# Strassen weight sums on VectorE, another order of products and later transposes in a decoder block's feed-forward

## The chip, the cores and the metric

The kernel runs on one core of one Trainium2 chip. The metric is the device time of one execution in microseconds; the time of a kernel is the median of its runs.

## The reference

A decoder block on x of 256 tokens x 2048 channels, all in float32: one input projection, a gated convolution and a gated linear attention, an output projection, a LayerNorm, and then the feed-forward with its own LayerNorm. The change lies in the feed-forward:

```python
x = layer_norm(DN_ALPHA * x + mix, ln1_g[l], ln1_b[l])
ff = jnp.square(jax.nn.relu(x @ w_ff_up[l])) @ w_ff_down[l]
x = layer_norm(DN_ALPHA * x + ff, ln2_g[l], ln2_b[l])
```

w_ff_up is 2048 x 8192, w_ff_down 8192 x 2048.

## The kernel before

**Split products.** Weights come as raw chunks of 512 KB (two blocks of 128 rows by 512 columns; pool rawp, 13 buffers). Each chunk is split into two parts that TensorE multiplies fast: ScalarE casts the high part (L108), VectorE subtracts it from the raw chunk for the low part (L109). The parts lie in one of five split buffers (pool hlp). Every product of two blocks is three matmuls of 512 columns (L153 to L155): high by high, high by low, low by high. Tokens come in two halves t of 128.

**Groups.** The 8192 hidden channels are done in eight groups of 1024. Group 0 is a plain product (`up_first`). Groups 1 to 7 (`up`) are a 2 x 2 Strassen form in Winograd's order: seven products instead of eight, on sums of the tokens' halves (s1, q, s3, s4, made once from x1 while group 0 runs) and sums of the weight quarters r11, r12, r21, r22. Each product has four steps of one weight chunk (28 steps a group, six matmuls a step), and accumulates into one of the PSUM banks a, b, c, d; three of the banks are used by two products, the second adding onto the first.

The list `plan` gives the order: what prepares the weight chunk, the left side, the bank, a DMA that adds to the chunk after its split (`then`), and what follows the last step (`end`). Before, the products come as r11 (bank a), r11+r12 by s1 (c), r21 (a), r11+r12+r22 by q (b), r12+r22 by s3 (d), r22 by s4 (c), r11+r12+r22+r21 (d). Two of the four weight sums are VectorE adds (`first_sum` L719, `third_sum` L724). The other two are made by DMAs from GpSimd's queue that add a weight quarter from HBM onto r11 in SBUF (`plus`, L728, four after the second product, four after the fourth).

**From bank to hidden block.** The `end_` functions combine banks with VectorE into u, v and x (L749, L750, L753, L758, L762), `out` applies relu on ScalarE (L737), `hidden` squares on VectorE (L653), and `put` transposes the block on TensorE (four transposes into a PSUM tile pt, L216) and splits the result into hT for the down product. `lag.soon` holds each such transposition back by a number of steps (two in `up`): `lag.after` is called after each up step and twice in each down chunk, once for each t.

**Down.** Each group's down product is 16 chunks of 12 matmuls; after every fourth chunk VectorE adds the two banks of the pair onto y (L802). Down chunks of the group before run between the up steps. A running count sets how many:

```python
downs, owed = all_downs(), -1.5
for g in range(1, NG):
    hTs.append(t8_pair(f"hT_{g}"))
    for _ in up(g, hTs[g]):
        owed += 4 / 7
        while owed >= 1:
            next(downs)
            owed -= 1
for _ in downs:
    pass
```

So 110 of the 112 down chunks of groups 0 to 6 run between up steps, 2 behind them, and then the last group's 16.

**Order of the work.** The program is traced in the order of the code. A planner with its own estimates of durations then lists each engine's instructions: at each point the earliest traced one that it holds to be ready. On the chip every engine goes through its list in that order. `prepare(s + 1)` stands before the split of step s, so a sum for the next step comes before the low part of this one. Loads all go through SP's queue, each as soon as a raw buffer is free. PSUM has six banks for products and two for transposes; a new tile takes a bank when its readers are done.

Of the kernel before, what the change touches and what calls it, by code (L numbers as in the profile page):

```python
# [12 lines left out]
AF = mybir.ActivationFunctionType  # L13
ALU = mybir.AluOpType
# [9 lines left out]
NB = 512  # L24
# [10 lines left out]
KC = 2  # L35
# [13 lines left out]
FIRST_WAIT = 6  # L49
WAIT_H = 2  # L50
WAIT_C = 8
C_B, C_C, C_U, C_Q, C_K, C_V, C_R, C_Z = 0, 1024, 2048, 3072, 3584, 4096, 5120, 6144

IN_COLS = [(C_Q, NB), (C_K, NB), (C_Z, RANK), (C_V, 2 * NB),
# [5 lines left out]
def hymba_block(ctx, tc, x, x_t, w_in, conv_w, conv_g, w_gate, gate_b, gla_g, w_out,  # L60
                ln1_g, ln1_b, w_up, w_down, ln2_g, ln2_b, out):
    nc = tc.nc
# [54 lines left out]
    def parts_of(raw, ncol, name):  # L117

        pool, tag = homes[0][homes[1] % len(homes[0])]
        homes[1] += 1  # L120
        hl = pool.tile([P, 2, KC, NB], F32R, tag=tag, name=f"hl_{name}")
        split(hl[:, 0, :, :ncol], hl[:, 1, :, :ncol], raw)
        return hl[:, 0], hl[:, 1]

    def piece(w, kt, at, ncol):

        words, n_kt = w
        start = P * (n_kt * at + kt * ncol)
        return words[start:start + P * KC * ncol].rearrange("(p k n) -> p k n", p=P, k=KC)

    def raw_chunk(w, kt, at, ncol, name):
        raw = rawp.tile([P, KC, NB], F32, tag="raw", name=f"raw_{name}")
        load(raw[:, :, :ncol], piece(w, kt, at, ncol))
        return raw[:, :, :ncol]
# [53 lines left out]
    def project(lagged, w, kts, at, ncol, lhs, done, name, ps=None, first=True, last=True,  # L188
                before=None, lags=None):

        ps = {} if ps is None else ps
        n = len(kts) // KC
        for i, chunk in enumerate(weight_chunks(w, kts, at, ncol, name)):
            if before is not None:
                before(i)

            if lags is not None:
                lagged.lag = lags[i]

            def work(t, i=i, chunk=chunk):  # L200
                if t not in ps:
                    ps[t] = acc_tile(f"ps_{name}_{t}")
                mm = products(ps[t], 0, ncol, chunk, lambda kt: lhs(kt, t), first and i == 0, last and i == n - 1)
                if i == n - 1 and last:
                    done(t, ps[t])
                return mm
            lagged.add(work)
        return ps
# [31 lines left out]
    def put(src, pair, j, t, name):  # L240
        transposed(src, pair[0][:, 4 * j:4 * j + 4, t * P:(t + 1) * P],
                   pair[1][:, 4 * j:4 * j + 4, t * P:(t + 1) * P], name)

    def part(pairs, kt, t):
        hi, lo = pairs[kt // 8]
        return hi[:, kt % 8, t * P:(t + 1) * P], lo[:, kt % 8, t * P:(t + 1) * P]
# [4 lines left out]
    with ExitStack() as p1:  # L251
# [97 lines left out]
        first = keep.tile([P, 1], F32, name="first")  # L349
# [127 lines left out]
        def conv_block(j):  # L477
# [26 lines left out]
            def done_b(t, ps):  # L504
# [8 lines left out]
                for g in range(4):  # L513
                    cols = slice(g * P, (g + 1) * P)
                    nc.vector.scalar_tensor_tensor(y[:, cols], y[:, cols], rstd[:, g:g + 1], cg[:, cols],
                                                   op0=ALU.mult, op1=ALU.mult)
                lag0.soon.append([1 + WAIT_C, lambda: put(y, mixT["conv"], j, t, f"c{j}{t}")])

# [29 lines left out]
    with ExitStack() as p2:  # L548
# [99 lines left out]
        def x1lhs(kt, t):  # L648
            return part(x1T, kt, t)

        def hidden(r, hT, i, t, name, wait):

            nc.vector.tensor_mul(r, r, r)  # L653
            lag.soon.append([wait, lambda: put(r, hT, i, t, name)])

        def up_first(hT):

            for i in range(GROUP // NB):
                def done(t, ps, i=i):
                    r = ht.tile([P, NB], F32, tag="relu", name=f"relu_0_{i}_{t}")  # L660
                    nc.scalar.activation(r, ps, AF.Relu)
                    hidden(r, hT, i, t, f"h0_{i}_{t}", 1 + WAIT_H)
                if i == 1:
                    homes[:] = [[(hlp, "hl")], 0]
                    lag.lag = 0
                project(lag, w_up, list(range(KT)), i * NB, NB, x1lhs, done, f"up0_{i}",
                        lags=LAGS if i == 0 else None, before=sums_ahead if i == 1 else None)
# [9 lines left out]
        KH = KT // 2  # L677
# [21 lines left out]
        def of_x1(half, t):  # L699
            return lambda kt: part(x1T, KH * half + kt, t)  # L700

        def of_sum(what):
            return lambda kt: (sums[what][:, 0, kt, :], sums[what][:, 1, kt, :])

        def up(g, hT):

            n1, n2 = g * GROUP, g * GROUP + NB
            r11, r12, r22 = {}, {}, {}

            def raw(at, half, j, name):  # L710
                return raw_chunk(w_up, KH * half + KC * j, at, NB, f"{name}_{g}_{j}")

            def first(j):
                r11[j] = raw(n1, 0, j, "r11")
                return r11[j]

            def first_sum(j):
                r12[j] = raw(n2, 0, j, "r12")
                nc.vector.tensor_add(r11[j], r11[j], r12[j])  # L719
                return r11[j]  # L720

            def third_sum(j):
                r22[j] = raw(n2, 1, j, "r22")
                nc.vector.tensor_add(r12[j], r12[j], r22[j])  # L724
                return r12[j]

            def plus(at):
                return lambda j: nc.gpsimd.dma_start(r11[j], piece(w_up, KH + KC * j, at, NB), accum_op=ALU.add)  # L728

            def tmp(name):  # L730
                return cp.tile([P, NB], F32, tag="c", name=f"{name}_{g}")

            banks, kept = {}, {}

            def out(x, i, t, where=None):
                r = x if where is None else where
                nc.scalar.activation(r, x, AF.Relu)  # L737
                hidden(r, hT, i, t, f"h{g}_{i}_{t}", 2)

            def end_1():  # L740
                kept["p1"] = tmp("p1")
                nc.scalar.copy(kept["p1"], banks["a"])

            def end_2():
                out(banks["a"], 0, 0, ht.tile([P, NB], F32, tag="relu", name=f"relu_{g}"))

            def end_6():
                kept["u"], kept["v"] = tmp("u"), tmp("v")
                nc.vector.tensor_sub(kept["u"], banks["b"], kept["p1"])  # L749
                nc.vector.tensor_sub(kept["v"], banks["c"], kept["u"])  # L750

            def end_7():
                nc.vector.tensor_sub(kept["v"], kept["v"], banks["d"])  # L753
                out(kept["v"], 1, 1)

            def end_3():
                x = tmp("x12")
                nc.vector.tensor_sub(x, kept["u"], banks["c"])  # L758
                out(x, 1, 0)

            def end_4():
                nc.vector.tensor_add(kept["u"], banks["d"], kept["u"])  # L762
                out(kept["u"], 0, 1)

            plan = [(first, of_x1(0, 0), "a", None, end_1),
                    (first_sum, of_sum("s1"), "c", plus(n2), None),
                    (lambda j: raw(n1, 1, j, "r21"), of_x1(1, 0), "a", None, end_2),
                    (lambda j: r11[j], of_sum("q"), "b", plus(n1), end_6),
                    (third_sum, of_sum("s3"), "d", None, end_7),
                    (lambda j: r22[j], of_sum("s4"), "c", None, end_3),  # L770
                    (lambda j: r11[j], of_x1(1, 1), "d", None, end_4)]
            n = KH // KC
            steps = [(p, j) for p in range(len(plan)) for j in range(n)]
            ready = {}

            def prepare(s):
                if s < len(steps):
                    p, j = steps[s]
                    ready[s] = plan[p][0](j)

            prepare(0)
            for s, (p, j) in enumerate(steps):
                _, lhs, bank, then, end = plan[p]
                prepare(s + 1)
                name = f"up{g}_{p}_{j}"
                parts = parts_of(ready.pop(s), NB, name)
                if then is not None:
                    then(j)
                if bank not in banks:
                    banks[bank] = acc_tile(f"ps_up{bank}_{g}")  # L790
                begun = any(q[2] == bank for q in plan[:p])
                mm = products(banks[bank], 0, NB, (list(range(KC * j, KC * j + KC)), *parts), lhs,
                              j == 0 and not begun, j == n - 1, more=begun)
                lag.after(mm)
                if j == n - 1 and end is not None:
                    end()
                yield
# [66 lines left out]
        downs = iter(())  # L864

        def all_downs():
            for g in range(NG - 1):
                yield from down(g, hTs[g])

        downs, owed = all_downs(), -1.5  # L870
        for g in range(1, NG):
            hTs.append(t8_pair(f"hT_{g}"))
            for _ in up(g, hTs[g]):
# [63 lines left out]
```

## Time and profile before

| | us |
|---|---|
| three runs | 1114.16, 1116.71, 1119.34 (median 1116.71) |
| the profiled execution | 1116.4, span 1114.7 |
| VectorE busy | 837.2, 75% of the span |
| ScalarE busy | 598.9, 54% |
| GpSimd busy | 63.9, 6% |
| stretch from the first product of group 1 to the last of group 7 | 440.2 to 1048.1 |

In the rows of the profile, hl_up and hl_dn are split up and down weights, raw_r and raw_dn the raw chunks, ps_upa to ps_upd the up banks, ps_dn the down banks, pt_h the tile of the transposes. PE is TensorE, PEld its weight loads, DVE VectorE, ACT ScalarE, POOL GpSimd, SP the queue of the loads. Rows in order of time have the start and the duration in us, then engine, line and operation; in brackets stands how long the engine sat idle before it and what ended that. Rows of waits have the waiting line, what it waited for, the total in us, the times and the longest. A matmul's duration reaches past the start of the next one, so the distance between starts is what one costs.

### The profile page before, as it was taken

Reading aid. Unit: us, or ns where it says so; the run is one execution under the profiler, and the core shown is the slowest. Engines: PE = TensorE matmul, PEld = TensorE weight load, DVE = VectorE, ACT = ScalarE, POOL = GpSimd, SP = SyncE. Lnnn points to the kernel's source line nnn. Section 1 sums busy time; section 2 is a strip of 40 time slices with the busy share of each in tenths; the row PEclk is TensorE's granted clock in tenths of the full one; section 3 lists DMA queues with packets and bytes.
Section 4 is the critical chain, followed back from the end, with each engine's and each line's share of the span. In section 5 each row is a group of like instructions: output and inputs, shape, how many; then the busy total and the mean of one; then the engine's idle time right before and its main releaser. Section 6 shows DMA issues by size and latency. Waiting matters only on the chain.

```text
span 1114.7 us, 13469 instructions
## 1 busy us (share of the span) xinstructions
PE 1071.6 (96%) x4914; PEld 896.2 (80%) x4914; DVE 837.2 (75%) x958; ACT 598.9 (54%) x695; POOL 63.9 (6%) x74
## 2 busy tenths in 40 slices
PE   9999999999999899999999999999989999989994
PEld 8998888888888778788878877877878877878884
DVE  6555558477655879689789789789879978968867
ACT  6476544436633545556546556556556655645531
POOL 0000000000000110100110110110110110010001
PEclk9999999999999999999999999999999999999998
DMA  9876267676766542997887888788698688688821
GB/s 337 306 254 206 83 209 256 206 225 216 263 225 194 164 159 107 252 258 244 242 228 267 226 228 285 201 239 296 165 252 297 168 251 300 174 232 273 278 63 75
DMA packets 76743, 248.06 MB, mean 223 GB/s; under 512 B 8003, under 2 KB 18259, under 8 KB 76422
## 3 DMA queue, kind: packets, MB, share of 16 engines
q1 hardware_dynamic: 65024, 207.78, 54.7%
q0 software_dynamic: 8064, 29.36, 14.5%
q10 hardware_dynamic: 3590, 10.08, 2.5%
q8 instruction: 38, 0.62, 0.2%
q14 instruction: 27, 0.22, 0.1%
HBM read 244.03 MB, written 3.15 MB: 222 GB/s over the span
## 4 chain that ended last, share of the span: by engine, by line
PE 68%; DVE 14%; DMA 12%; issue 4%; ACT 2%; SPq 0%; DVEq 0%; ACTq 0%
DMA raw_dn<-in_w_ff_down_dram 6%; PE ps_dn L154 6%; PE ps_dn L153 6%; PE ps_dn L155 6%; DMA raw_r<-in_w_ff_up_dram 5%; DVE hl_up L109 5%; DVE hl_dn L109 3%; PE ps_p L155 3%; PE ps_p L153 3%; PE ps_p L154 3%; PE ps_o L155 2%; PE ps_o L154 2%; PE ps_o L153 2%; PE ps_upd L154 2%; PE ps_upd L153 2%
## 5 line engine op out<-in xcount | busy, mean ns | idle before, releaser
L108 ACT CAST hl_up<-raw_r 128x1024 fp32r<-128x1024 f32 x196 | 205.6, 1052 | 107.6 <-PE ps_dn L155 51.5
L109 DVE TENSOR_TENSOR hl_up<-raw_r,hl_up 128x1024 fp32r<-128x1024 f32 x196 | 237.4, 1219 | 30.9 <-ACT hl_up L108 28.4
L108 ACT CAST hl_dn<-raw_dn 128x1024 fp32r<-128x1024 f32 x128 | 134.8, 1053 | 142.8 <-PE ps_dn L155 77.1
L109 DVE TENSOR_TENSOR hl_dn<-raw_dn,hl_dn 128x1024 fp32r<-128x1024 f32 x128 | 156.1, 1220 | 54.4 <-ACT hl_dn L108 53.1
L154 PE MATMUL ps_dn<-hl_dn,hT_hi 128*128 128x512 f32 x496 | 193.5, 390 | 0.5 <-DVE hl_dn L109 0.5
L153 PE MATMUL ps_dn<-hl_dn,hT_hi 128*128 128x512 f32 x496 | 193.3, 390 | 0.0
L155 PE MATMUL ps_dn<-hl_dn,hT_lo 128*128 128x512 f32 x496 | 193.1, 389 | 0.0
L154 PEld LDWEIGHTS ps_dn<-hl_dn,hT_hi 128*128 128x128 f32 x496 | 93.1, 188 | 20.8 <-DVE hl_dn L109 1.3
L153 PEld LDWEIGHTS ps_dn<-hl_dn,hT_hi 128*128 128x128 f32 x496 | 93.1, 188 | 19.8
L155 PEld LDWEIGHTS ps_dn<-hl_dn,hT_lo 128*128 128x128 f32 x496 | 93.1, 188 | 19.4
L728 POOL DMA_DIRECT2D raw_r<-in_w_ff_up_dram x56 | 48.5, 866 | 561.7 <-DVE hl_up L109 530.0
L109 DVE TENSOR_TENSOR hl_p<-raw_p,hl_p 128x824 fp32r<-128x824 f32 (+1 forms) x40 | 40.3, 1016 | 33.4 <-ACT hl_p L108 31.7
L109 DVE TENSOR_TENSOR hl_o<-raw_o,hl_o 128x1024 fp32r<-128x1024 f32 x32 | 38.8, 1222 | 32.9 <-ACT hl_o L108 32.5
L108 ACT CAST hl_o<-raw_o 128x1024 fp32r<-128x1024 f32 x32 | 33.4, 1056 | 45.2 <-PE ps_o L155 31.7
L153 PE MATMUL ps_p<-hl_p,xT_hi 128*128 128x412 f32 (+1 forms) x160 | 56.2, 351 | 0.2 <-ACT xT_hi L108 0.2
L154 PE MATMUL ps_p<-hl_p,xT_hi 128*128 128x412 f32 (+1 forms) x160 | 56.2, 351 | 0.0
L155 PE MATMUL ps_p<-hl_p,xT_lo 128*128 128x412 f32 (+1 forms) x160 | 55.8, 349 | 0.3
L724 DVE TENSOR_TENSOR raw_r<-raw_r,raw_r 128x1024 f32<-128x1024 f32 x28 | 34.2, 1222 | 28.0 <-DMA raw_r<-in_w_ff_up_dram 28.0
L108 ACT CAST hl_p<-raw_p 128x824 fp32r<-128x824 f32 (+1 forms) x40 | 35.1, 885 | 27.1 <-PE ps_p L155 21.4
L154 PE MATMUL ps_upa<-hl_up,x1T_hi 128*128 128x512 f32 x112 | 44.1, 394 | 0.0
L153 PE MATMUL ps_upc<-hl_up,sum_s 128*128 128x512 f32 x112 | 44.1, 394 | 0.0
L153 PE MATMUL ps_upa<-hl_up,x1T_hi 128*128 128x512 f32 x112 | 43.7, 391 | 0.0
(281 smaller groups left out, 2168.2 us busy)
## 6 DMA issues: line engine op xcount, KB each, us to landing
raw_dn<-in_w_ff_down_dram SPq DMA_DIRECT2D x128, 512.0 KB, 5.0
raw_r<-in_w_ff_up_dram SPq DMA_DIRECT2D x112, 512.0 KB, 5.3
raw_r<-in_w_ff_up_dram POOLq DMA_DIRECT2D x56, 512.0 KB, 8.1
raw_o<-in_w_out_dram SPq DMA_DIRECT2D x32, 512.0 KB, 3.5
raw_p<-in_w_in_dram SPq DMA_DIRECT2D x24, 412.0 KB, 5.7
raw_c<-in_w_in_dram SPq DMA_DIRECT2D x16, 512.0 KB, 3.7
raw_u<-in_w_in_dram SPq DMA_DIRECT2D x16, 512.0 KB, 4.3
raw_b<-in_w_in_dram SPq DMA_DIRECT2D x16, 512.0 KB, 4.2
```

The source lines that it names most:

```text
L108: queued("act", lambda: nc.scalar.copy(hi, src))
L109: queued("dve", lambda: nc.vector.tensor_sub(lo, src, hi.bitcast(F32)))
L153: nc.tensor.matmul(ps[:, :ncol], ah, whi[:, j, cols], start=f, stop=False, skip_group_check=more)
L154: nc.tensor.matmul(ps[:, :ncol], ah, wlo[:, j, cols], start=False, stop=False, skip_group_check=more)
L155: nc.tensor.matmul(ps[:, :ncol], al, whi[:, j, cols], start=False, stop=e, skip_group_check=more)
L724: nc.vector.tensor_add(r12[j], r12[j], r22[j])
L728: return lambda j: nc.gpsimd.dma_start(r11[j], piece(w_up, KH + KC * j, at, NB), accum_op=ALU.add)
```

## The change

- The accumulating DMAs (`plus`) are gone. The second and fourth weight sum become VectorE adds: `second_sum` adds r22 onto r11, `fourth_sum` adds r21. VectorE makes 16 adds a group instead of 8.
- The products come in another order: r11 (a), r11+r12 by s1 (c), r12+r22 by s3 (d), r11+r12+r22 by q (b), r22 by s4 (c), r21 (a), r11+r12+r22+r21 (d). `end_7` is merged into `end_6`, which now runs after the fourth product; `end_2` runs after the sixth.
- Where a block lies in SBUF, relu and square are one VectorE instruction (the larger of x and 0, times x) in place of a ScalarE relu and a VectorE multiply. Where it comes straight from a bank (`end_2` and group 0), both are done by ScalarE.
- Transposes in `up` wait six calls instead of two.
- The running count of the down chunks starts at -6 instead of -1.5: 105 chunks run between up steps, 7 behind them. In group 1 the first follows step 13 instead of step 5. In the groups after it down chunks follow steps 1, 2, 4, 6, 8, 9, 11, 13, 15, 16, 18, 20, 22, 23, 25 and 27.

```diff
+WAIT_UP = 6
+BEHIND = 6
...
-        def hidden(r, hT, i, t, name, wait):
-            nc.vector.tensor_mul(r, r, r)
+        def hidden(r, x, hT, i, t, name, wait):
+            if r is x:
+                nc.vector.scalar_tensor_tensor(r, x, 0.0, x, op0=ALU.max, op1=ALU.mult)
+            else:
+                nc.scalar.activation(r, x, AF.Relu)
+                nc.scalar.activation(r, r, AF.Square)
             lag.soon.append([wait, lambda: put(r, hT, i, t, name)])
...
-                    nc.scalar.activation(r, ps, AF.Relu)
-                    hidden(r, hT, i, t, f"h0_{i}_{t}", 1 + WAIT_H)
+                    hidden(r, ps, hT, i, t, f"h0_{i}_{t}", 1 + WAIT_H)
...
-            def plus(at):
-                return lambda j: nc.gpsimd.dma_start(r11[j], piece(w_up, KH + KC * j, at, NB), accum_op=ALU.add)
+            def second_sum(j):
+                nc.vector.tensor_add(r11[j], r11[j], r22[j])
+                return r11[j]
+
+            def last(j):
+                r21[j] = raw(n1, 1, j, "r21")
+                return r21[j]
+
+            def fourth_sum(j):
+                nc.vector.tensor_add(r11[j], r11[j], r21[j])
+                return r11[j]
...
             def out(x, i, t, where=None):
-                r = x if where is None else where
-                nc.scalar.activation(r, x, AF.Relu)
-                hidden(r, hT, i, t, f"h{g}_{i}_{t}", 2)
+                hidden(x if where is None else where, x, hT, i, t, f"h{g}_{i}_{t}", WAIT_UP)
...
                 nc.vector.tensor_sub(kept["u"], banks["b"], kept["p1"])
                 nc.vector.tensor_sub(kept["v"], banks["c"], kept["u"])
-
-            def end_7():
                 nc.vector.tensor_sub(kept["v"], kept["v"], banks["d"])
                 out(kept["v"], 1, 1)
...
-            plan = [(first, of_x1(0, 0), "a", None, end_1),
-                    (first_sum, of_sum("s1"), "c", plus(n2), None),
-                    (lambda j: raw(n1, 1, j, "r21"), of_x1(1, 0), "a", None, end_2),
-                    (lambda j: r11[j], of_sum("q"), "b", plus(n1), end_6),
-                    (third_sum, of_sum("s3"), "d", None, end_7),
-                    (lambda j: r22[j], of_sum("s4"), "c", None, end_3),
-                    (lambda j: r11[j], of_x1(1, 1), "d", None, end_4)]
+            plan = [(first, of_x1(0, 0), "a", end_1),
+                    (first_sum, of_sum("s1"), "c", None),
+                    (third_sum, of_sum("s3"), "d", None),
+                    (second_sum, of_sum("q"), "b", end_6),
+                    (lambda j: r22[j], of_sum("s4"), "c", end_3),
+                    (last, of_x1(1, 0), "a", end_2),
+                    (fourth_sum, of_x1(1, 1), "d", end_4)]
...
-        downs, owed = all_downs(), -1.5
+        downs, owed = all_downs(), -BEHIND
```

More of the change, by code (lines that the diff above doesn't have):

```diff
@@ L707, in up @@
             n1, n2 = g * GROUP, g * GROUP + NB
-            r11, r12, r22 = {}, {}, {}
+            r11, r12, r21, r22 = {}, {}, {}, {}
             def raw(at, half, j, name):
@@ L782, in up @@
             for s, (p, j) in enumerate(steps):
-                _, lhs, bank, then, end = plan[p]
+                _, lhs, bank, end = plan[p]
                 prepare(s + 1)
@@ L786, in up @@
                 parts = parts_of(ready.pop(s), NB, name)
-                if then is not None:
-                    then(j)
                 if bank not in banks:
```

## The prediction

> **What bounds the kernel now.** I read the page's busy shares first, then the waits of TensorE and VectorE in the stretch where up groups 1 to 7 run between the down chunks (440 to 1048 us), then that stretch in one row, then the instructions around one stall in order of time.
>
> ```profile
> PE 1071.6 (96%) x4914; PEld 896.2 (80%) x4914; DVE 837.2 (75%) x958; ACT 598.9 (54%) x695; POOL 63.9 (6%) x74
> L728 POOL DMA_DIRECT2D raw_r<-in_w_ff_up_dram x56 | 48.5, 866 | 561.7 <-DVE hl_up L109 530.0
> q0 software_dynamic: 8064, 29.36, 14.5%
> ...
> PE pt_h L216 <- DVE relu L653: 17.7, 7, 3.8
> PE pt_h L216 <- DVE v L653: 2.3, 4, 0.7
> PE ps_dn L154 <- DVE hl_dn L109: 0.5, 2, 0.3
> ...
> DVE hl_dn L109 <- ACT hl_dn L108: 43.4, 33, 5.3
> DVE raw_r L724 <- DMA raw_r<-in_w_ff_up_dram: 28.0, 17, 3.0
> DVE hl_up L109 <- ACT hl_up L108: 27.8, 26, 2.3
> ...
> ACT hl_dn L108 <- PE ps_dn L155: 57.5, 41, 1.9
> ACT hl_up L108 <- PE ps_dn L155: 51.5, 39, 1.7
> ```
>
> TensorE bounds the stretch, with VectorE some way behind. TensorE is never held by missing weights to speak of (0.5 us); it is held once per group, seven times, by the transposes of the first finished block (end_2's), which wait for VectorE's squaring at L653: 17.7 us in all, the longest 3.8. VectorE's own largest waits are for ScalarE's casts, and these wait for TensorE to free a split buffer: that is back-pressure, not a limit. Only the 28.0 us of L724 are a real lack: r22 has not landed.
>
> The stretch in one row (us, then busy PE, PEld, DVE, ACT, POOL with counts, granted clock, DMA share, GB/s), and TensorE in order of time around one stall, in a dense run, and after a slightly shorter stall:
>
> ```profile
> 440.20:1048.10 607.90, 587.46 (x2603) 481.51 (x2602) 504.40 (x504) 352.37 (x369) 48.49 (x56) 0.99 0.82 240
> ...
> 559.10 0.39 PE L155 MATMUL ps_dn<-hl_dn,hT_lo 128*128 128x512 f32 x1
> 561.95 1.03 PE L216 MATMUL pt_h<-ident,relu 128*128 128x128 f32 x4 [2.46 <-DVE relu L653]
> 562.63 0.78 PE L153 MATMUL ps_upb<-hl_up,sum_q 128*128 128x512 f32 x1
> 565.34 0.44 PE L153 MATMUL ps_upb<-hl_up,sum_q 128*128 128x512 f32 x1
> ...
> 570.88 0.39 PE L153 MATMUL ps_dn<-hl_dn,hT_hi 128*128 128x512 f32 x1
> 589.92 0.39 PE L153 MATMUL ps_upc<-hl_up,sum_s 128*128 128x512 f32 x1
> 590.60 0.63 PE L216 MATMUL pt_h<-ident,v 128*128 128x128 f32 x4
> 591.53 0.39 PE L155 MATMUL ps_upc<-hl_up,sum_s 128*128 128x512 f32 x1
> ...
> 911.40 0.63 PE L216 MATMUL pt_h<-ident,relu 128*128 128x128 f32 x4 [2.33 <-DVE relu L653]
> 911.79 0.48 PE L153 MATMUL ps_upb<-hl_up,sum_q 128*128 128x512 f32 x1
> 913.96 0.39 PE L153 MATMUL ps_upb<-hl_up,sum_q 128*128 128x512 f32 x1
> ```
>
> Between 570.88 and 589.92 lie 84 products (four down chunks of 12, six up chunks of 6): 0.2267 us from start to start. An up chunk is 1.36 us, a down chunk 2.72. Four transposes delay what follows by 0.47 (from 590.60 the third product starts after 0.93 instead of 0.45). So the stretch holds 7 x 28 x 6 + 110 x 12 = 2496 products, 565.8 us, and 28 sets of transposes, 13.2: 579.0 us of work. The rest of its 607.9 is 28.9: 17.7 + 2.3 + 0.5 = 20.5 waited and 8.4 left. Where the 8.4 are is seen after the stall of 2.46: six products from 562.63 to 565.34 took 2.71 us instead of 1.36, half speed. After the stall of 2.33 nine products took 2.17 (0.24 each): full speed. So a stall from about 2.4 us costs some 1.7 us more, one of 2.3 nothing.
>
> The Trainium skill (TensorE: Matmul & The Clock Gate, "HAM oscillation") puts the limit at idle gaps of more than about 3.4 us. The rows differ: 2.46 us was enough. By the page only the 3.8 us stall would be charged and a new stall under 3.4 us would be free: the sum below would lack its 1.7, 1103 instead of 1105.
>
> **The change, part by part.**
>
> *Transposes later, squares elsewhere.* The block that stalls now (end_2) gets relu and square from ScalarE, so VectorE's queue is out of its chain, and all transposes come six products' steps later (some 8 us of TensorE work) instead of two. ScalarE is at 352 of 607.9 us; one square more per group and three relus fewer cost nothing there. In up_first four squares move the same way, beside the products: nothing. The stalls and half-speed windows go: at most 28.9 us.
>
> *56 accumulating DMAs out, 56 adds in.* POOL loses its only work in the stretch. SP issues the same 112 loads: r22 comes two products earlier and r21 three later, past down loads on the same queue. Held raw buffers are 8 to 9 of 13 in products two to four, as they are now. 29.4 MB and q0's 14.5% of the DMA engines go. VectorE is what pays. Its pitch in a dense run:
>
> ```profile
> 612.00 1.22 DVE L719 TENSOR_TENSOR raw_r<-raw_r,raw_r 128x1024 f32<-128x1024 f32 x1
> 613.14 1.22 DVE L109 TENSOR_TENSOR hl_dn<-raw_dn,hl_dn 128x1024 fp32r<-128x1024 f32 x1
> 614.27 0.68 DVE L109 TENSOR_TENSOR hT_lo<-pt_h,hT_hi 128x512 fp32r<-128x512 f32 x1
> 614.87 1.21 DVE L109 TENSOR_TENSOR hl_up<-raw_r,hl_up 128x1024 fp32r<-128x1024 f32 x1
> 616.01 1.22 DVE L719 TENSOR_TENSOR raw_r<-raw_r,raw_r 128x1024 f32<-128x1024 f32 x1
> 617.27 1.23 DVE L109 TENSOR_TENSOR hl_up<-raw_r,hl_up 128x1024 fp32r<-128x1024 f32 x1
> ```
>
> An instruction over 1024 columns takes 1.135 us of the engine (start to start), one over 512 takes 0.60; durations overlap by 0.08. New VectorE work: 504.4 + 56 x 1.135 = 63.6, less 7 multiplies (4.2), and less 5 down chunks that leave the stretch (below; 5.7 + 1.2): 556.9 us. The three fused max-and-multiply per group take the place of three multiplies of the same size: nothing.
>
> *Down chunks later.* The count starts at -6 instead of -1.5, so 105 chunks instead of 110 run inside the stretch and 7 instead of 2 behind it. Total TensorE work is the same; the stretch falls to 579.0 - 5 x 2.72 = 565.4 and 13.6 go behind it, where VectorE needs 1.135 of every 2.72 us. Cost: none by itself. But in group 1 the first down chunk now follows step 13, so products two and three run alone: VectorE needs 2 x 1.135 for each 1.36 of TensorE, 8 x 0.91 = 7.3 us short, against a lead of five split buffers, 6.8. I take 3 us (0.5 if the lead is whole, 7.3 if none).
>
> *The order of products.* This is the part that can bite. Product five (s4) now accumulates into bank c directly behind product four, and end_6 must first read c (v = c - u, after u = b - p1). Today bank c is touched again only eight steps later. Between product four and five stands one down chunk (after step 16). Where u and v stand today, three of the seven groups (last product into b, then u, then v):
>
> ```profile
> 574.73 0.39 PE L155 MATMUL ps_upb<-hl_up,sum_q 128*128 128x512 f32 x1
> 577.27 0.68 DVE L749 TENSOR_TENSOR u<-ps_upb,p 128x512 f32<-128x512 f32 x1
> 579.27 0.68 DVE L750 TENSOR_TENSOR v<-ps_upc,u 128x512 f32<-128x512 f32 x1
> ...
> 746.54 0.39 PE L155 MATMUL ps_upb<-hl_up,sum_q 128*128 128x512 f32 x1
> 750.94 0.68 DVE L749 TENSOR_TENSOR u<-ps_upb,p 128x512 f32<-128x512 f32 x1
> 752.67 0.68 DVE L750 TENSOR_TENSOR v<-ps_upc,u 128x512 f32<-128x512 f32 x1
> ...
> 1014.06 0.39 PE L155 MATMUL ps_upb<-hl_up,sum_q 128*128 128x512 f32 x1
> 1015.40 0.68 DVE L749 TENSOR_TENSOR u<-ps_upb,p 128x512 f32<-128x512 f32 x1
> 1017.37 0.68 DVE L750 TENSOR_TENSOR v<-ps_upc,u 128x512 f32<-128x512 f32 x1
> ```
>
> TensorE would want bank c at 0.23 + 2.72 us after the last row of b; v ends 2.3, 3.9 and 1.05 us after that. If the down chunk covered all, the cost would be 0; as today, 1.05 to 3.9 us per group, with half speed on top from 2.4. I take 1.05: the larger two stand behind L724 adds that waited for DMA, at the very place where the accumulating DMAs ran. 7 x 1.05 = 7.4, and one half-speed window, 1.7. Behind the waiting product five stand all TensorE's later products; VectorE meanwhile refills its lead. Four up banks are now live in product four, so a new pair of down banks (step 13) needs the old pair's adds within 4.1 us; the u row of 746.54 (3.9 + 0.68) says 0 to 0.5 per group. I take 0.
>
> **The sum.** By TensorE: 565.4 + 7.4 + 1.7 + 3 = 577.5. By VectorE: 556.9, plus hand-overs of 0.12 as at 616.01 (1.26 instead of 1.135) on about one in five of 400 long instructions, 10, plus a third of L724's DMA waits, 10, plus waits for b and c, 3: 580. The two stand so close that each pays some of the other's waits; an estimate of 3 more gives 583. With the 13.6 behind the stretch it is 596.6 against 607.9: 11.3 us less. The profiled execution took 1116.4 us (span 1114.7), the median of the runs is 1116.71, so both give **1105 us**.
>
> **Rivals.**
>
> *Nothing takes the stalls' place.* The down chunk covers v and VectorE keeps up: 579.0 in all, 1116.4 - 28.9 = 1087.5, up to 1095 with some of the terms. For it: no accumulating DMAs. Against: VectorE at 556.9 of 565.4, 98%.
>
> *The stall moves from the transposes to bank c.* v late as in the 574.73 and 746.54 rows: 7 x 2.7 = 19, four half-speed windows 7, group 1's 3: 565.4 + 29 + 13.6 = 608, no change, 1111 to 1122. For it: two of three rows. Against: they follow DMA waits.
>
> *VectorE becomes the bound: slower.* It decides from the point where VectorE idles 607.9 - 13.6 - 556.9 = 37 us in the stretch; today it idles 103.5, of which 28.0 for DMA and the rest mostly back-pressure, which goes when its lead is gone. If the DMA waits stay (28) with hand-overs (10) and waits for b (7 x 0.95 as in the 1014.06 rows, 7), it idles 45: 1116.4 + 8 = 1124, and more where loads come later.
>
> The Trainium skill (VectorE: DVE Perf Modes, "The DRAIN you can't avoid") speaks for this one: the next operation would start only when the pipe is empty. By that rule each would cost its whole duration: with 413 long ones (196 + 105 splits, 112 adds) and some 138 short ones, 413 x 1.22 + 138 x 0.68 = 598 us, and with the 13.6 the change would give 1120. The rows above differ: starts lie 1.13 to 1.14 apart under durations of 1.22.
>
> **Chances.** My forecast (1095 to 1111) 0.42; nothing takes the stalls' place 0.16; the stall moves to bank c 0.22; VectorE bounds 0.20. Half a per cent, 5.6 us, is about what a measurement of this kernel can tell from no change. Faster by more: 0.42 + 0.16 = 0.58; within: 0.21; slower: 0.21. Range 1090 to 1122: it cuts a part of the first rival's low end and the slow rival's upper part.
>
> **What would show it.** No POOL DMAs, 56 more long VectorE instructions, DVE near 95% in the stretch; no TensorE wait for relu at the transposes; instead a wait of the first product of ps_upc in product five on v (L750 of today), about 1 us, seven times; DMA share well under 0.82. Wrong would be: that wait over 2.4 us with half-speed products behind it; TensorE waiting for hl_up or hl_dn many times (VectorE bounds); adds waiting for r12 or r22 as long as L724 does now.

## The result and the profile after

| | before | after |
|---|---|---|
| median of 4 runs, us | 1116.68 | 1087.12 (1086.87 to 1087.62) |
| ratio | | 0.9737, 95% interval 0.9719 to 0.9755 |
| profiled execution, us | 1116.4, span 1114.7 | 1086.87, span 1085.1 |
| granted clock, mean | 0.988 | 0.995 |
| stretch of groups 1 to 7, us | 607.9 | 567.4 |

29.6 us less, where 11 were forecast; the time lies below the range. It is near the first rival, "nothing takes the stalls' place" (1087.5).

Of two kernels below ("the same, with later transposes" and "2 long VectorE instructions more a group") the one profiled execution took over 3000 us: the ratios leave it out, and no rows of these two are shown.

From the page after, the busy shares and the one queue of the loads (GpSimd's has no transfers left); from its waits, the longest of TensorE's (it lies in LayerNorm 1, ahead of the stretch) and VectorE's two largest in the stretch; and the stretch in one row (us, busy PE, PEld, DVE, ACT, POOL with counts, clock, DMA share, GB/s). Line numbers are two or more higher than before; L111 is L109 of before.

```profile
PE 1062.4 (98%) x4914; PEld 892.2 (82%) x4914; DVE 888.8 (82%) x1003; ACT 594.0 (55%) x685; POOL 15.4 (1%) x18
q1 hardware_dynamic: 65024, 207.78, 58.2%
...
PE pt_x L218 <- DVE y L595: 2.8, 1, 2.8
...
DVE hl_up L111 <- ACT hl_up L110: 8.9, 7, 1.5
DVE hl_dn L111 <- ACT hl_dn L110: 4.8, 7, 1.2
...
440.13:1007.56 567.43, 567.29 (x2554) 468.38 (x2552) 549.87 (x545) 342.09 (x354) 0.00 (x0) 1.00 0.62 202
```

Not one wait of TensorE is left in the stretch: it is busy 567.29 of 567.43 us at full clock. VectorE does 45 instructions more and is at 97%. No add waits for a DMA. The stretch is 40.5 us shorter, and what follows it is 10.9 longer (77.5 against 66.6). The prediction moved five down chunks behind the stretch, 13.6 us; it was four, because in the trace of before the stretch holds 109 chunks (1308 down products up to the last up product) and not the 110 of the program. The stretch after is 2.0 us longer than the 565.4 of pure work that the prediction counted.

Bank c, the place that the prediction feared, in group 2 of the kernel after (last product into b, the first one behind it, first product of s4; u and v on VectorE):

```profile
552.57 0.39 PE L157 MATMUL ps_upb<-hl_up,sum_q 128*128 128x512 f32 x1
552.80 0.39 PE L155 MATMUL ps_dn<-hl_dn,hT_hi 128*128 128x512 f32 x1
556.20 0.39 PE L155 MATMUL ps_upc<-hl_up,sum_s 128*128 128x512 f32 x1
...
553.42 0.68 DVE L761 TENSOR_TENSOR u<-ps_upb,p 128x512 f32<-128x512 f32 x1
555.15 0.68 DVE L762 TENSOR_TENSOR v<-ps_upc,u 128x512 f32<-128x512 f32 x1
```

v ends at 555.83, 3.03 us after TensorE could have gone on; 15 down products stand between (3.40 us), three more than the one chunk that the program's order puts there: the planner listed some earlier. Over the seven groups v ends 2.6 to 3.1 us after that point, and the products between take 2.9 to 3.4.

### The profile page after: what moved, and what is told of

It is laid out like the page before. It is cut to its first block, busy times and chain, and to the rows that moved or that the text cites. A ratio compares the mean times of both kernels' runs of the same rounds, so it can differ in the third digit from the quotient of the medians.

```text
span 1085.1 us, 13282 instructions
## 1 busy us (share of the span) xinstructions
PE 1062.4 (98%) x4914; PEld 892.2 (82%) x4914; DVE 888.8 (82%) x1003; ACT 594.0 (55%) x685; POOL 15.4 (1%) x18
## 4 chain that ended last, share of the span: by engine, by line
PE 91%; DVE 6%; ACT 1%; DMA 1%; issue 1%; DVEq 0%
PE ps_dn L156 10%; PE ps_dn L157 10%; PE ps_dn L155 10%; PE ps_p L157 3%; PE ps_p L156 3%; PE ps_p L155 3%; PE ps_o L157 2%; PE ps_o L156 2%; PE ps_o L155 2%; PE ps_upa L155 2%; PE ps_upc L155 2%; PE ps_upa L157 2%; PE ps_upa L156 2%; PE ps_upc L156 2%; PE ps_upc L157 2%; PE ps_upd L155 2%
## 5 line engine op out<-in xcount | busy, mean ns | idle before, releaser
L111 DVE TENSOR_TENSOR hl_up<-raw_r,hl_up 128x1024 fp32r<-128x1024 f32 x196 | 236.8, 1218 | 9.8 <-ACT hl_up L110 9.3
L111 DVE TENSOR_TENSOR hl_dn<-raw_dn,hl_dn 128x1024 fp32r<-128x1024 f32 x128 | 156.0, 1219 | 22.5 <-ACT hl_dn L110 21.6
L111 DVE TENSOR_TENSOR hl_p<-raw_p,hl_p 128x824 fp32r<-128x824 f32 (+1 forms) x40 | 40.3, 1017 | 33.1 <-ACT hl_p L110 31.4
L111 DVE TENSOR_TENSOR hl_o<-raw_o,hl_o 128x1024 fp32r<-128x1024 f32 x32 | 38.8, 1223 | 32.8 <-ACT hl_o L110 32.5
L155 PE MATMUL ps_upc<-hl_up,sum_s 128*128 128x512 f32 x112 | 44.3, 396 | 0.0
L157 PE MATMUL ps_upa<-hl_up,x1T_lo 128*128 128x512 f32 x112 | 43.7, 390 | 0.0
L156 PE MATMUL ps_upc<-hl_up,sum_s 128*128 128x512 f32 x112 | 43.7, 390 | 0.0
```

Source lines behind the costliest of these rows:

```text
L111: queued("dve", lambda: nc.vector.tensor_sub(lo, src, hi.bitcast(F32)))
L155: nc.tensor.matmul(ps[:, :ncol], ah, whi[:, j, cols], start=f, stop=False, skip_group_check=more)
L156: nc.tensor.matmul(ps[:, :ncol], ah, wlo[:, j, cols], start=False, stop=False, skip_group_check=more)
L157: nc.tensor.matmul(ps[:, :ncol], al, whi[:, j, cols], start=False, stop=e, skip_group_check=more)
```

## The experiments

All times are medians in us; ratios are to the kernel before on the same chip.

| kernel | us | ratio, 95% interval |
|---|---|---|
| before + spacing alone | 1119.27 | 1.0017 (1.0000 to 1.0034) |
| before + squares alone | 1132.21 | 1.0111 (1.0075 to 1.0146) |
| before + spacing and squares, old order | 1119.46 | 1.0030 (1.0009 to 1.0052) |
| after, sums 2 and 4 by DMA again | 1087.21 | 0.9721 (0.9707 to 0.9736) |
| after, old spacing | 1092.11 | 0.9767 (0.9752 to 0.9781) |
| after, square of end_2 on VectorE | 1089.00 | 0.9747 (0.9733 to 0.9762) |
| after, no down chunk traced between products four and five | 1087.67 | 0.9735 (0.9718 to 0.9752) |
| after, 2 long VectorE instructions more a group | 1089.16 | 0.9745 (0.9728 to 0.9761) |
| after, 6 more a group | 1116.10 | 0.9992 (0.9982 to 1.0003) |
| after, 11 raw buffers | 1091.45 | 0.9767 (0.9743 to 0.9792) |
| before, no accumulating DMAs | 1087.16 | 0.9729 (0.9708 to 0.9751) |
| the same, with later transposes | 1086.85 | 0.9727 (0.9703 to 0.9752) |
| before, only the four behind product two | 1110.39 | 0.9938 (0.9922 to 0.9955) |
| before, only the four behind product four | 1097.85 | 0.9825 (0.9810 to 0.9840) |
| before, the 56 as plain loads | 1088.02 | 0.9737 (0.9723 to 0.9752) |

**Spacing alone.** In the kernel before:

```diff
-                hidden(r, hT, i, t, f"h{g}_{i}_{t}", 2)
+                hidden(r, hT, i, t, f"h{g}_{i}_{t}", 6)
-        downs, owed = all_downs(), -1.5
+        downs, owed = all_downs(), -6
```

> The kernel before with only the spacing changed: transposes six calls later instead of two, down chunks counted from -6 instead of -1.5. Order of products, accumulating DMAs and squares as before. Theory A (the gain is the end of the seven stalls at end_2's transposes, and the spacing alone ends them): TensorE's 20.5 us of waits and 8.4 us of half speed go, 1088 to 1092 us. Theory B (VectorE ran late because of the accumulating DMAs, and only their removal ends the stalls): VectorE's adds at L724 still wait about 28 us for DMAs, and half or more of the stall stays, 1100 to 1112 us.

**Squares alone.** `hidden` and `out` of the change, all else as before.

> The kernel before with only relu and square changed: one VectorE instruction for the blocks in SBUF, ScalarE for both where a block comes from a bank. Spacing two calls, order and DMAs as before. Theory A2 (the stall is VectorE's queue in front of end_2's square; ScalarE's square would end 0.6 us after its relu, which is before TensorE asks for it): the wait of 17.7 us falls below 3 and nearly all half speed goes, 1089 to 1096 us. Theory A (only the spacing ends the stalls): the wait moves to ScalarE and stays above 1 us a group, 1103 to 1115 us.

**Spacing and squares, in the old order** with the accumulating DMAs: the whole change without its order and sums.

> The changed kernel's squares, spacing and down count, but the order of products and the accumulating DMAs of before: all of the change except order and sums. Spacing alone gave 1119 us and squares alone 1132; the new order with the sums left to the DMAs 1087. Theory C (r22 lands late in the old order and TensorE stalls behind VectorE's L724 wherever that shows): 1115 to 1130 us, L724 waiting 30 us or more for DMAs. Theory A, saved (both spacing and squares are needed to end the stall): 1087 to 1095 us.

1119, 1132 and 1119 us: none gains, and in the first two neither theory's time was met. TensorE's and VectorE's waits in the stretch (waiting line, what for, us in total, times, longest), of the three in turn, with ScalarE's wait for down loads in the second:

```profile
PE ps_dn L154 <- DVE hl_dn L109: 21.3, 8, 5.9
DVE raw_r L724 <- DMA raw_r<-in_w_ff_up_dram: 48.9, 20, 8.2
...
PE pt_h L216 <- DVE v L654: 13.2, 7, 2.1
PE ps_upb L154 <- DVE hl_up L109: 11.8, 7, 2.2
DVE raw_r L727 <- DMA raw_r<-in_w_ff_up_dram: 36.4, 21, 3.6
ACT hl_dn L108 <- DMA raw_dn<-in_w_ff_down_dram: 79.5, 17, 8.9
...
PE ps_dn L154 <- DVE hl_dn L109: 20.3, 11, 5.6
DVE raw_r L727 <- DMA raw_r<-in_w_ff_up_dram: 53.5, 25, 7.9
```

The transposes no longer stall (with spacing), and the same 20 us stand elsewhere in the group, where TensorE runs out of split weights. With spacing alone each of the seven long stalls (1.6 to 5.9 us) comes 2.4 us after an L724 add that waited 4.0 to 8.2 us for r22. So the stall at the transposes was only the place where VectorE's lateness showed; what made VectorE late was still there. Theory A fell; the saved form of it, that both edits together are needed, fell with the third run. With the squares alone TensorE stalls at two places a group: 2.4 us after an L727 add (L724 of before) that waited 3.2 to 3.6 us for r22, and, from group 1 to 6, some 12 us after a cast that waited 7.0 to 8.9 us for a down load. ScalarE waits 79.5 us for down loads in that run, 47.3 in the kernel before. Why these loads come so much later there stays open.

**The new order, with the two sums left to the DMAs.** In the kernel after:

```diff
-                    (first_sum, of_sum("s1"), "c", None),
+                    (first_sum, of_sum("s1"), "c", plus(n2), None),
...
-                    (second_sum, of_sum("q"), "b", end_6),
+                    (lambda j: r11[j], of_sum("q"), "b", plus(n1), end_6),
...
-                    (fourth_sum, of_x1(1, 1), "d", end_4)]
+                    (lambda j: r11[j], of_x1(1, 1), "d", None, end_4)]
```

> The changed kernel with the second and fourth weight sum made by accumulating DMAs again, issued behind the splits of products two and four; all else as changed (order of products, spacing, squares). VectorE has 56 long instructions fewer (63.6 us). Theory A (VectorE at 550 of 567 us was no bound, and DMAs were no bound before): 1086 to 1090 us, as the changed kernel. Theory B: the accumulating DMAs bring TensorE stalls back, above 1095 us.

1087.21, as the kernel after. The stretch (row of 440.13 to 1007.56 as above), VectorE's wait for r22 and ScalarE's for down loads in this run:

```profile
440.13:1007.56 567.43, 567.43 (x2555) 468.31 (x2554) 494.20 (x488) 340.60 (x355) 48.53 (x56) 1.00 0.85 254
...
DVE raw_r L729 <- DMA raw_r<-in_w_ff_up_dram: 16.9, 6, 4.2
ACT hl_dn L110 <- DMA raw_dn<-in_w_ff_down_dram: 29.4, 8, 5.9
```

TensorE never waits in the stretch, although VectorE still waits 16.9 us for r22, ScalarE 29.4 for down loads, and the DMA engines are at 0.85. The down loads even take longer to land than in the kernel before (median 6.4 us against 5.1 between 440 and 1010). So in this order late loads cost nothing, and VectorE's adds brought nothing and cost nothing. Why this order bears them is not shown. VectorE has 56 us less to do here than in the kernel after, which leaves it time to catch up, but hardly less than in the kernel before (494.2 against 504.4). The new spacing and squares are in this run too; the new order with accumulating DMAs and without them was not run.

**The accumulating DMAs left out, in the old order.** These kernels leave r22 and r21 out of r11's sums; they show what the DMAs cost. Before, with old spacing and squares, then with later transposes and down chunks counted from -6:

```diff
-                if then is not None:
-                    then(j)
```

> The kernel before with its 56 accumulating DMAs left out, so that r22 and r21 are missing from r11's sums; all else, the old order too, as before. Theory D (the DMA engines are too full where r22 is loaded): L724's waits for DMA fall from 28.0 us to a few, the stalls at end_2's transposes to a third, 1088 to 1098 us. Theory E (r22 is late because of its place in the old order, with 13 raw buffers of which r11, r12 and r21 hold 8 to 10): the waits stay above 15 us, 1105 to 1117 us.

> The same without the accumulating DMAs, with transposes six calls later and down chunks counted from -6. Theory D: no DMA wait and no early transposes are left, 1086 to 1090 us. Theory E: L724's waits stay near the 48.9 us that the later transposes alone showed, 1108 to 1119 us.

1087.16 and 1086.85. With the old order, the old spacing and the old squares, the whole gain is there once these 56 DMAs are gone. The window of before's stretch (440.20 to 1048.10; in this run it also takes in work from behind the stretch, which ends some 30 us earlier) and the waits, of the first of the two:

```profile
440.20:1048.10 607.90, 607.90 (x2737) 501.21 (x2737) 524.84 (x528) 367.28 (x382) 0.00 (x0) 1.00 0.62 200
...
DVE raw_r L724 <- DMA raw_r<-in_w_ff_up_dram: 2.6, 7, 0.6
...
ACT hl_dn L108 <- DMA raw_dn<-in_w_ff_down_dram: 2.2, 4, 0.5
```

The last row is the one that was missed. In the kernel before it reads:

```profile
ACT hl_dn L108 <- DMA raw_dn<-in_w_ff_down_dram: 47.3, 23, 5.5
```

Theory D holds in its main point: without these DMAs the loads are in time and the stalls go. Its other point, that it is the load of r22 which counts, is taken up by the next runs. Theory E falls.

**Which of them, and why.** Only the four behind product two (r21 is missing from r11's sums), only the four behind product four (r22 is missing), and all 56 as plain loads, which overwrite r11:

```diff
 (first_sum, of_sum("s1"), "c", plus(n2), None)     # only these four: plus(n1) -> None
 (lambda j: r11[j], of_sum("q"), "b", plus(n1), end_6)   # only these four: plus(n2) -> None
...
-... piece(w_up, KH + KC * j, at, NB), accum_op=ALU.add)
+... piece(w_up, KH + KC * j, at, NB))
```

> The kernel before with only the first four accumulating DMAs of each group (r22 onto r11 behind product two); the four that add r21 behind product four are left out of the computation. If those behind product four are the ones in the way (they are issued while r22 is loaded for L724): L724's waits fall below 5 us, 1086 to 1090 us. If the first four are: 1105 us or more.

> The kernel before with only the second four (r21 onto r11 behind product four); the four behind product two are left out of the computation. If these are the ones in the way: L724 still waits 15 us or more for DMAs and TensorE stalls at end_2's transposes, 1105 to 1117 us. If it takes both sets: 1087 to 1098 us.

> The kernel before with the 56 DMAs from GpSimd's queue as plain loads into r11 that overwrite it, so r11's sums are not made. If what hurts is the adding (reading and writing SBUF beside the bytes from HBM): they take about half the DMA engines' time, L724's waits fall below 10 us, 1087 to 1095 us. If it is the 29 MB, or GpSimd's queue as such: 1110 to 1118 us.

Waits of TensorE, VectorE and ScalarE with the first four only, then with the second four only:

```profile
PE pt_h L216 <- DVE relu L653: 17.2, 7, 3.4
DVE raw_r L724 <- DMA raw_r<-in_w_ff_up_dram: 10.6, 7, 2.1
ACT hl_dn L108 <- DMA raw_dn<-in_w_ff_down_dram: 29.9, 14, 5.2
...
PE pt_h L216 <- DVE v L653: 5.2, 7, 1.0
DVE raw_r L724 <- DMA raw_r<-in_w_ff_up_dram: 27.9, 20, 3.6
ACT hl_dn L108 <- DMA raw_dn<-in_w_ff_down_dram: 22.0, 12, 3.5
```

My expectation was the wrong way round: L724's 27.9 us of waits come with the second four, where TensorE waits 6.8 us (5.2 at the transposes, 1.6 for hl_dn) and the run is about 10 us longer than with plain loads. The stall at end_2's transposes comes with the first four, with 10.6 us at L724; TensorE waits 17.2 us, and the run is about 22 us longer. They act in another way. In the kernel before, one group (the load's issue on SP's queue, ScalarE's cast of that chunk, VectorE's split of it):

```profile
537.86 0.33 SPq L112 DMA_DIRECT2D raw_dn<-in_w_ff_down_dram  x1
...
546.83 1.05 ACT L108 CAST hl_dn<-raw_dn 128x1024 fp32r<-128x1024 f32 x1 [3.93 <-DMA raw_dn<-in_w_ff_down_dram]
...
547.91 1.22 DVE L109 TENSOR_TENSOR hl_dn<-raw_dn,hl_dn 128x1024 fp32r<-128x1024 f32 x1 [3.76 <-ACT hl_dn L108]
```

A down load issued at 537.86, among four accumulating DMAs (issued from 530.91 to 539.27), takes 8.7 us to land and is used at 546.83; ScalarE stands 3.93 us and behind it VectorE 3.76, and 14 us later the square that end_2's transposes need comes 2.46 us late. It is so in all seven groups: such a wait of ScalarE, 2.1 to 5.5 us, lies some 15 us ahead of the stall, and the longer it is the longer the stall (1.70 us behind the shortest, 3.82 behind the longest). Between the two lies a wait of L724 of 1.2 to 1.9 us; what each contributes was not separated. What slows the load (page of before, then of the run with plain loads: issues on GpSimd's queue with us to landing, and that queue's packets, MB and share of the DMA engines; before's share, 14.5%, stands in the prediction):

```profile
raw_r<-in_w_ff_up_dram POOLq DMA_DIRECT2D x56, 512.0 KB, 8.1
...
raw_r<-in_w_ff_up_dram POOLq DMA_DIRECT2D x56, 512.0 KB, 4.9
q0 software_dynamic: 8064, 29.36, 8.4%
```

The same 29.36 MB from the same queue as plain loads take 8.4% of the engines instead of 14.5% and cost next to nothing (1088.02 against 1087.16 without them). It is the adding, not the bytes or the queue. How the adding delays the other loads inside the DMA engines no run shows. The Trainium skill (DMA: Bandwidth & Descriptors, "SWDGE vs HWDGE vs iDMA") ties accumulating transfers to GpSimd's queue; what they do to plain loads beside them is measured by these runs.

**Was bank c covered by luck?** Down chunks counted from -6.5, so that none is traced between product four and five:

```diff
-BEHIND = 6
+BEHIND = 6.5
```

> The changed kernel with the down chunks counted from -6.5 instead of -6: again 105 inside the stretch, but they follow steps 15 and 17 and not 16, so product five follows product four directly. v was done 3.0 us after the last product into bank b could have been followed. If the down chunk between the two was what covered v: seven stalls of about 3 us and half speed after most of them, 1108 to 1122 us. If the planner puts other products there: 1087 to 1092 us.

1087.67. Last product into b, next product, first one of s4:

```profile
553.55 0.39 PE L157 MATMUL ps_upb<-hl_up,sum_q 128*128 128x512 f32 x1
553.78 0.39 PE L155 MATMUL ps_dn<-hl_dn,hT_hi 128*128 128x512 f32 x1
557.63 0.39 PE L155 MATMUL ps_upc<-hl_up,sum_s 128*128 128x512 f32 x1
```

17 down products stand between, where the program's order has none. The planner fills the gap.

**How much room has VectorE?** The low part subtracted twice at some steps of each group:

```diff
+                if s in (0, 18):    # or (0, 5, 10, 15, 20, 25)
+                    nc.vector.tensor_sub(parts[1], src, parts[0].bitcast(F32))
```

> The changed kernel with the low part of a split subtracted twice in 2 of the 28 steps of each group (steps 0 and 18): 14 long VectorE instructions more, 15.9 us. VectorE then has 549.9 + 15.9 = 565.8 us of work in a stretch of 567.4. If VectorE's limit is its work by the distance between starts (1.135 us each), with nearly no idle: 1087 to 1092 us. If each instruction costs its whole duration, VectorE already was the bound and each one adds 1.22: 1104 us. By the prediction's 23 us of idle that VectorE can't avoid: about 1108 us.

> The same with the low part subtracted twice in 6 of 28 steps (0, 5, 10, 15, 20, 25): 42 long instructions more, 47.7 us, VectorE 597.6 us against TensorE's 567.4. If VectorE bounds from there on: 1087 + 30 = 1117 us, up to 1128 with short TensorE stalls that are charged with half speed. If its lead and the stretches around it take up part: 1105 to 1115 us.

1089.16 and 1116.10: 14 instructions more (15.9 us by 1.135 each) cost about 2, 42 (47.7 us) cost 29. With six more a group VectorE is the bound, busy all the time (TensorE has 579.91 of the same stretch):

```profile
440.10:1035.00 594.90, 579.91 (x2550) 465.14 (x2549) 591.63 (x584) 335.24 (x353) 0.00 (x0) 1.00 0.56 189
```

VectorE idled 17.6 us in the stretch of after (567.43 less 549.87); 47.7 less 17.6 is 30, near the 29 measured. So VectorE's limit is its work at 1.135 us per long instruction, and in this run it was filled to 99% (591.63 of 594.90).

**Spacing, squares and buffers in the new order.**

> The changed kernel with the old spacing: transposes two calls later, down chunks counted from -1.5. By theory A2 end_2 stays without a stall, but v's four VectorE instructions end 6.3 us after product four (they are spread over four splits) and its transposes are asked for after about 2.7 us; and with this count no down chunk stands between product four and five, so bank c is asked for 3.0 us before v has read it. 3.5 to 6 us per group and half speed on top: 1112 to 1135 us. If the planner fills both gaps with down products: 1087 to 1095 us.

> The changed kernel with the square of end_2 (and of group 0) on VectorE again, behind ScalarE's relu; spacing of six calls and all else as changed. Theory A (the spacing ends the stall, whoever squares): 1086 to 1090 us. If it was the square on ScalarE: a wait for VectorE of 1 us or more per group, above 1093 us.

> The changed kernel with 11 raw buffers instead of 13. Theory E (what counts is how many raw buffers are left for loads ahead): with 3 instead of 5 beside the 8 held ones, loads of r12 and r22 come late, VectorE waits for DMAs 20 us or more, 1095 to 1125 us. Theory D (bandwidth, which is at 0.62 here): 1087 to 1091 us.

With the old spacing (`WAIT_UP = 2`, `BEHIND = 1.5`) the new order takes 1092.11 instead of 1087.12: the transposes of u wait six times.

```profile
PE pt_h L218 <- DVE u L656: 4.1, 6, 1.3
```

The stalls expected at v and bank c (25 us or more) are not there; the planner filled them. With the squares of end_2 and of group 0 on VectorE it is 1089.00, with no TensorE wait above 1 us in the stretch. Neither edit is where the gain came from; in the new order the spacing is worth some 5 us. With 11 raw buffers the time is 1091.45: ScalarE waits 41.1 us for down loads (0.6 in the kernel after), but TensorE under 2 us in the stretch. So two buffers less cost about 4 us and not the 8 or more that theory E needs; where the rest of the 4 us goes was not followed.

## Why the prediction was wrong

- **The step of the sum that failed.** The sum went by VectorE: 580 us, and 3 more for mutual waiting, 583 for the stretch. It took 567.4, and TensorE was busy in all but 0.14 of them. VectorE's work was put at 556.9 us; 549.9 was measured, for nearly the same count (546 instructions worked out, 545 in the row). The 23 us of idle time added to it (hand-overs 10, waits for DMA 10, waits for b and c 3) were 17.6, the mutual waiting of 3 was nothing, and none of it held TensorE. TensorE's own line was too high as well, by the 12.1 us put down for bank c and group 1.
- **What bounds the kernel now.** The 28.9 us of waits and half speed were near the 29.6 that went. But I read VectorE's 43.4 us of waits for ScalarE's casts as back-pressure by quoting only ScalarE's waits for TensorE. ScalarE's 47.3 us for down loads stand in the same view and lead to the same stall. "Only the 28.0 us of L724 are a real lack" is the reading that failed, and with it the mechanism: the idle terms and bank c were priced by rows of before, in which late loads held VectorE.
- **Transposes later, squares elsewhere: the stalls go.** They went, by another edit. Spacing and squares gain nothing in the old order. What freed the kernel is either leaving out the accumulating DMAs in the old order (1087.16) or the new order, with new spacing and squares, in spite of them (1087.21).
- **56 DMAs out, 56 adds in.** I kept a third of L724's waits, 10 us, although the DMAs go; no add waits for a DMA in the stretch. That the DMAs themselves cost the old order some 30 us (ratio 0.9729 without them) is nowhere in the sum.
- **The order of products.** 7 x 1.05 and 1.7 for bank c came out as 0. Two things were left out. With loads in time u starts 0.2 to 0.65 us after the last product into b could be followed (0.62 in the rows above) instead of 1.1 to 4.2; so in five of the seven groups v ends after 2.62 us and the one down chunk (2.72) would have covered it. And the planner lists down products ahead of product five when v isn't ready.
- **Group 1's 3 us**: 0.14 us at most, which is all that TensorE idled in the stretch.
- **The rivals.** Bank c as the new stall fell with two runs; VectorE as the bound is real only from some 17 us more work on, as the runs with two and six more show. By whole durations VectorE would have been the bound at 598 us of work already in the kernel after; the row of after has 549.87 in a stretch of 567.43.

With the terms that failed taken out, the sum gives 565.4 + 13.6 = 579.0 for the stretch and the moved chunks, the first rival's 1087.5. Measured, it is 567.4 + 10.9 = 578.3. That the rival comes within 0.4 us of the median is in part luck: 2.0 too little in the stretch and 2.7 too much behind it all but cancel. Its own reasons hold (v is covered, VectorE keeps up, the accumulating DMAs are gone), but the end of the stalls, which it takes over from the part on transposes and squares, has another cause.

## What to carry to other kernels

A stall is priced where it shows, but its cause is followed back: VectorE's wait for ScalarE was ScalarE's wait for a load, and a load was late because of transfers that nobody waited for. A resource that is slack on average (the DMA engines, at 0.82) can still set the time when a load with little lead is issued among a few slow transfers; in another order of work the same slow transfers cost nothing. And an edit that removes the visible wait is worth testing alone: here it moved the 20 us to another place and gained nothing.

## What the runs showed of the hardware

Whether a stall is followed by half speed is not settled by its length. In the run with squares alone, a stall of 2.10 us left full speed, one of 2.12 did not (next products 0.23 and 0.43 us apart); of the six such stalls of 2.06 to 2.12 us there, every other one was followed by a granted clock of 0.67 to 0.68 over some 5 us, the others by 1.00:

```profile
683.59 0.63 PE L216 MATMUL pt_h<-ident,v 128*128 128x128 f32 x4 [2.10 <-DVE v L654]
685.22 0.39 PE L153 MATMUL ps_upc<-hl_up,sum_s 128*128 128x512 f32 x1
685.45 0.39 PE L154 MATMUL ps_upc<-hl_up,sum_s 128*128 128x512 f32 x1
...
592.92 0.63 PE L216 MATMUL pt_h<-ident,v 128*128 128x128 f32 x4 [2.12 <-DVE v L654]
595.03 0.63 PE L153 MATMUL ps_upc<-hl_up,sum_s 128*128 128x512 f32 x1
595.46 0.63 PE L154 MATMUL ps_upc<-hl_up,sum_s 128*128 128x512 f32 x1
```

The same wait of 2.82 us in LayerNorm 1 was free in the kernel after and charged in the run with only the second four (granted clock 0.77 in a stretch of 8 us; first row after, second row that run):

```profile
378.00:386.00 8.00, 4.55 (x23) 3.04 (x21) 7.89 (x10) 5.47 (x7) 3.83 (x3) 1.00 0.35 124
378.00:386.00 8.00, 5.18 (x22) 4.25 (x21) 7.89 (x9) 5.20 (x7) 4.51 (x3) 0.77 0.43 131
```

The Trainium skill (TensorE: Matmul & The Clock Gate, "What's actually happening") has the clock set by how busy TensorE was in a window that is free-running and does not start with the kernel. That agrees with the rows: equal stalls would fare differently by where in the window they fall. So "from 2.4 us" in the prediction was too sharp.
